# First projections for all 512 tokens in one pass, and the queries of three token blocks together

## The chip, the cores and the metric

The kernel runs on one core of a Trainium2 chip. The core has a TensorE for matrix products (PE in the profile), a VectorE (DVE), a ScalarE (ACT), a GpSimd (POOL), a SyncE (SP) that issues most transfers, and 16 DMA engines. The metric is the time of one execution on the device in microseconds (us).

## The reference, cut to what matters

512 tokens (T) of 1024 features (D) pass through two layers, all in float32. The first layer:

```python
mod = silu(c) @ w_ada + b_ada                       # 6 x 1024 modulations, one vector for all tokens
shift1, scale1, gate1, shift2, scale2, gate2 = split(mod, 6)
h = rms_norm(x, g1) * (1 + scale1) + shift1
q_g, k_g, v_g, a_lr, r_g, q_s, k_s, v_s = split(h @ w_in)    # the "first projections"
o_gla = rms_norm(gated_linear_attention(q_g, k_g, v_g, log_sigmoid(a_lr @ w_a + b_a) / 16)) * silu(r_g)
o_swa = rms_norm(sliding_window_attention(q_s, k_s, v_s))
x = x + gate1 * (concat(o_gla, o_swa) @ w_out)

h2 = rms_norm(x, g2) * (1 + scale2) + shift2
q = h2 @ w_peer_q                                   # 8 heads, two half queries of 128
s1, s2 = q_half1 @ keys_1.T, q_half2 @ keys_2.T     # 128 scores each
# 16 best of s1, 16 best of s2, then the 16 best of their 256 sums: 16 of 16,384 experts for each head
a = gelu(h2 . u_tab[expert]);  x = x + gate2 * sum(gate * a * v_tab[expert])
x = rms_norm(x, final_g)
```

The second layer takes x on: a norm, projections, differential and stick-breaking attention, an output projection, and a gated feed-forward layer. The output is x of all tokens.

## The kernel before

The tokens are four blocks of 128 (0 to 3), with features on the partitions and tokens along the free dimension. Two ways of computing the experts stand side by side. For blocks 0 and 3 (`SPARSE`), GpSimd gathers the chosen experts' rows, 128 of the up table (`peer_u`) and 128 of the down table (`peer_v`) per block, each gathered row 128 x 1024 floats (0.52 MB); VectorE consumes each row with one multiply-and-sum (`sparse`, 1191). For blocks 1 and 2 (`DENSE`), TensorE multiplies the 256 tokens with the whole tables, 128 steps each (`dense_u` 1314, `dense_v` 1381); the gates go into a 128 x 128 matrix per token (`gate_matrix`, 1258) that passes through DRAM.

A float32 product runs on TensorE as it stands, or as a "pair": ScalarE writes a rounded high part (`whi`), VectorE the rest (`wlo`, "a cut"), and `mm3` (393) makes three faster products of them. In the trace a float32 product leaves two records, a product of a pair one each.

The order of work on each engine is made as the program is built. `Model` (74) keeps a rough clock of the engines, and `Weaver` (225) always takes the next step of that generator whose last step ends first by it; a generator can wait for a key, for data, or stand back by a number of us. The constants from 52 on set how far parts stand back: `WIN` the projections of block 0, `SWL` the sliding window, `GLL` the linear attention of the later blocks. The product i of the up table for i of at least `AHEAD + SPILL` (17 + 32) waits for product i - `AHEAD` of the down table; the first `SPILL` activations go out to DRAM (`act_d`) and come back (`aR`) when the down table wants them. All instructions bear line 221, where a wrapper records them, so tiles tell them apart.

The front of the program, in which the change lies: `ada` (533) sums 48 groups of 128 modulations on VectorE, each over a 128 x 1024 piece of `w_ada`; 16 must be there before `first_norm` (574) can make its operand. The first projections (`w_in`, 604) run twice over 19 weight tiles: for block 0 in float32 (128 columns), then for blocks 1 to 3 in pairs (384 columns), so the weights are loaded twice. `gla` (705) runs the linear attention for block 0, for 1 and 2, and for 3; each has eight levels that end in two masked copies (`COPY_PREDICATED`), and ends in outputs `yT<-orb,b_w`, for which the gates (`silu` of r_g) must be there. `swa` (864) is the sliding window, `w_out` (977) the output projection, of block 0 and of blocks 1 to 3. `queries` (998) makes the second norm, the 16 tiles of queries and the scores: for block 0, for blocks 1 and 2 (256 columns), and for block 3, each in float32 and each with its own load of the weights. `topk_first` and `topk_second` (1084, 1099) search the scores; after block 0's the gathers of its experts begin.

The two lines that run all this:

```python
gla(pat, 0, 1, 0), [late(GLL)], gla(pat, 1, 3, 1), gla(pat, 3, 4, 1)   # of the call at 1511
W.run(posts(), topk(), gate_matrix(), dense_u(), dense_v(), until=("XD", "X0"))
```

## Time and profile before

| | |
|---|---|
| median of 3 runs | 2233.68 us (2230.89 to 2234.12) |
| span of the profiled execution | 2237.0 us |
| TensorE busy | 2040.0 us, 91% |
| VectorE busy | 1787.4 us, 80% |
| ScalarE busy | 968.8 us, 43% |
| GpSimd busy | 628.3 us, 28% |

The profile is of one execution of its own; its span is 3.3 us above the median of the timed runs. The busy shares are averages over stages that differ: where the program waits is seen only when the span is cut into stretches, and there for each engine's busy time, for the granted clock of TensorE and for the share of the time in which the DMA engines move data. A row of the time line is one instruction, or a run of like ones (x16), with its start, its duration, its engine, and the tiles out and in; what stands in brackets is how long the engine had been idle and what ended that. A row of the chain of waits is a piece of the path that ended last.

### The profile page before, as it was taken

The numbers are of one execution on the slowest core, as the hardware profiler recorded it, in microseconds if no ns is written. First come the engines' busy times: TensorE is split into PE (matmuls) and PEld (weight loads), VectorE is DVE, ScalarE is ACT, GpSimd is POOL, SyncE is SP. The second block draws the span as 40 slices with busy tenths as digits, with TensorE's granted clock in tenths as the row PEclk, the third lists the DMA queues.
The fourth block names the chain that finished last, engine by engine and source line by source line (L and its number), as shares of the span: only waits on it lengthen the run. The fifth ranks groups of instructions, "written<-read, shape, count | busy, mean of one in ns | idle before, by whom it ended". The sixth has DMA issues, their size and how long they took to land.

```text
span 2237.0 us, 36437 instructions
## 1 busy us (share of the span) xinstructions
PE 2040.0 (91%) x13373; PEld 1865.9 (83%) x13373; DVE 1787.4 (80%) x3723; ACT 968.8 (43%) x1824; POOL 628.3 (28%) x523
## 2 busy tenths in 40 slices
PE   2889899798999888999999999699997999999998
PEld 2778776687899788999999999587865999999887
DVE  6845897698999878888888697988978999932487
ACT  1331432212577533444444544445454333344376
POOL 0000223432112244333333133455522655400000
PEclk9899999799999988999999999899997999999999
DMA  9853447898898999999999798798855999954387
GB/s 367 335 207 129 160 146 240 278 326 312 281 325 304 358 337 321 366 344 354 343 374 330 241 380 292 272 326 289 286 178 159 371 354 364 356 166 139 130 306 268
DMA packets 227570, 638.32 MB, mean 285 GB/s; under 512 B 21264, under 2 KB 71712, under 8 KB 227392
## 3 DMA queue, kind: packets, MB, share of 16 engines
q1 hardware_dynamic: 153664, 367.54, 46.4%
q0 software_dynamic: 73728, 268.47, 34.1%
q8 instruction: 105, 1.72, 0.3%
q14 instruction: 73, 0.60, 0.1%
HBM read 611.54 MB, written 24.38 MB: 284 GB/s over the span
## 4 chain that ended last, share of the span: by engine, by line
PE 72%; DVE 11%; DMA 10%; ACT 3%; issue 3%; SPq 1%; POOL 0%; ACTq 0%; DVEq 0%; POOLq 0%
PE b_mm L221 46%; PE b_dacc L221 12%; PE b_w L221 6%; PE b_z L221 3%; DMA wraw<-peer_v 3%; DVE row L221 3%; DVE wlo L221 2%; DMA row<-w_up 1%; DMA aR<-act_d 1%; PE b_osb L221 1%; ACT whi L221 1%; SPq L221 1%; DMA row<-w_ada 1%; PE b_s L221 1%; DVE xT L221 1%
## 5 line engine op out<-in xcount | busy, mean ns | idle before, releaser
L221 POOL DMA_INDIRECT row<-peer_u,eU x256 | 311.4, 1217 | 845.7 <-DVE sm L221 250.1
L221 POOL DMA_INDIRECT row<-peer_v,eU x256 | 314.1, 1227 | 475.8 <-DVE vacc L221 204.6
L221 PE MATMUL b_mm<-u,whi 128*128 128x384 f32 x1216 | 327.4, 349 | 20.3 <-DMA sgt<-sgt 10.0
L221 PE MATMUL b_mm<-h,whi 128*128 128x256 f32 (+2 forms) x1632 | 329.9, 298 | 2.3 <-ACT whi L221 2.3
L221 DVE SCALAR_TENSOR_TENSOR vacc<-row,dots,vacc 128x1024 f32<-128x1024 f32 x254 | 324.7, 1278 | 3.9 <-DMA row<-peer_v,eU 3.5
L221 PE MATMUL b_dacc<-ghi,vhi 128*128 128x256 f32 x1024 | 296.0, 289 | 28.8 <-ACT ghi L221 28.7
L221 DVE SCALAR_TENSOR_TENSOR row<-row,h2n 128x1024 f32<-128x1024 f32 x256 | 309.8, 1218 | 13.1 <-DMA row<-peer_u,eU 13.0
L221 PE MATMUL b_dacc<-glo,vhi 128*128 128x256 f32 x1024 | 296.8, 290 | 2.4 <-DVE glo L221 1.8
L221 PE MATMUL b_dacc<-ghi,vlo 128*128 128x256 f32 x1024 | 294.7, 288 | 0.0
L221 PEld LDWEIGHTS b_mm<-h,whi 128*128 128x128 f32 (+1 forms) x1632 | 258.6, 190 | 8.9 <-issue 5.0
L221 PEld LDWEIGHTS b_mm<-u,whi 128*128 128x128 f32 x1216 | 223.5, 193 | 41.0 <-ACT u L221 20.4
L221 PE MATMUL b_mm<-h,wlo 128*128 128x256 f32 (+2 forms) x816 | 239.8, 294 | 8.7 <-DVE wlo L221 8.7
L221 PEld LDWEIGHTS b_dacc<-ghi,vhi 128*128 128x128 f32 x1024 | 201.1, 196 | 30.6 <-ACT ghi L221 30.5
L221 PE MATMUL b_mm<-u,wlo 128*128 128x384 f32 x608 | 209.0, 344 | 12.3 <-DVE wlo L221 12.3
L221 ACT ACTIVATE whi<-wraw 128x1024 fp32r<-128x1024 f32 (+5 forms) x143 | 128.0, 896 | 198.7 <-PE b_mm L221 112.2
L221 ACT ACTIVATE vhi<-wraw 128x1024 fp32r<-128x1024 f32 x128 | 136.0, 1063 | 169.5 <-PE b_dacc L221 100.6
L221 PEld LDWEIGHTS b_dacc<-glo,vhi 128*128 128x128 f32 x1024 | 201.1, 196 | 5.0 <-DVE glo L221 5.0
L221 PEld LDWEIGHTS b_dacc<-ghi,vlo 128*128 128x128 f32 x1024 | 201.6, 197 | 0.0
L221 PE MATMUL b_mm<-h,uraw 128*128 128x256 f32 x720 | 171.4, 386 | 4.6 <-DMA uraw<-peer_uT 3.2
L221 PEld LDWEIGHTS b_mm<-h,wlo 128*128 128x128 f32 (+1 forms) x816 | 156.2, 191 | 11.1 <-DVE wlo L221 10.3
L221 DVE TENSOR_TENSOR vlo<-wraw,vhi 128x1024 fp32r<-128x1024 f32 x128 | 156.1, 1220 | 10.5 <-PE b_dacc L221 9.9
L221 PEld LDWEIGHTS b_mm<-h,uraw 128*128 128x128 f32 x720 | 135.1, 195 | 21.7 <-issue 3.6
(350 smaller groups left out, 3787.2 us busy)
## 6 DMA issues: line engine op xcount, KB each, us to landing
uraw<-peer_uT SPq DMA_DIRECT2D x128, 512.0 KB
wraw<-peer_v SPq DMA_DIRECT2D x128, 512.0 KB
wraw<-w_in SPq DMA_DIRECT2D x60, 512.0 KB
row<-w_ada SPq DMA_DIRECT2D x48, 512.0 KB
wraw<-w_peer_q SPq DMA_DIRECT2D x32, 512.0 KB
gt<-gate_d SPq DMA_DIRECT2D x16, 1024.0 KB
gate_d<-stg SPq DMA_DIRECT2D x16, 896.0 KB
row<-w_in SPq DMA_DIRECT2D x24, 512.0 KB
```

The source lines that it names most:

```text
L221: return f(*args, **kw)
```

## The change

1. **First projections once.** x is loaded whole (two transfers of 1 MB) ahead of the modulations' weights, not block 0 first. `ada` takes the modulations in the order scale, shift of chunk 0, of chunk 1, and so on; as a pair is summed, `first_norm` makes that chunk (128 features) of the operand for all 512 tokens. `w_in` runs once over its 19 tiles, in pairs of 512 columns, and the weights are loaded once. Its first four tiles are cut in advance, their parts standing in room that belongs to q, k and v of the linear attention, and go chunk by chunk into four banks. `first_norm`, `gla` and `swa` lose the argument that told the two passes apart.
2. **Queries together.** `w_out(0, 1)`, `queries(0, 1)`, `w_out(1, 4)` and `queries(1, 4)` follow each other in one generator. The queries of blocks 1 to 3 are made in one go, in pairs of 384 columns (`pairs`, new), and w_peer_q is loaded twice, not three times. Block 3's scores are copied to SBUF. `topk_first` takes a group of heads of one block at a time; `topk_second` works in two halves of the heads.
3. **Order.** `AHEAD` 9 and `SPILL` 48 (57 in sum, before 49); `SWL` and `GLL` 0; `dense_u` waits for the output projection and takes pairs only once the queries are done (`post`) and VectorE is free by the model. The model's costs for TensorE and VectorE are other ones. `o1`, `o2` of the gate matrix have 2 buffers, not 3.

Counted over the program: 18 fewer loads of `w_in`, 16 fewer of `w_peer_q`, 8 fewer transfers of `w_out`; 16 more activations out to `act_d` and back; 55 steps of the up table in float32 and 73 in pairs, before 45 and 83. Gathered rows that VectorE has consumed when the last output projection stands, when the first product of the down table does, and at the end of the tables: before 47, 134 and 300, now 1, 103 and 284. Comments are gone from the file.

```diff
-AHEAD = 17
-SPILL = 32
+AHEAD = 9
+SPILL = 48
...
-    def w_in(b0, b1):
-        c, n = slice(128 * b0, 128 * b1), 128 * (b1 - b0)
+    def w_in():
...
+        pss = [bank(k) for k in ("mm", "mm", "s", "s")]
+        for kc in range(KC):
+            yield need(f"n{kc}")
+            for i in range(4):
+                mm3(pss[i], [x[:, kc] for x in spl[i]], (h1[:, 0, kc], h1[:, 1, kc]), kc == 0, kc == KC - 1)
+            yield at(M.free["PE"])
...
+    def pairs(tiles, xs, p, raw, n):
...
+        for i, (_, m, ev, *keys) in enumerate(tiles):
+            for k in keys:
+                yield need(k)
+            cut_hi(i + 1)
+            w = spl.pop(i)
+            ps = bank("mm")[:m, :n]
+            for kc in range(KC):
+                mm3(ps, (w[0][:, kc], w[1][:, kc]), (xs[0][:, kc], xs[1][:, kc]), kc == 0, kc == KC - 1)
+                if kc == 3:
+                    yield at(M.free["PE"])
+                    cut_lo(i + 1)
+                    load(i + 4)
...
-        yield need("Y")
+        yield need("x1")
+        stY.close()
...
-            if i < NE and ("G" in W.done or i >= AHEAD + SPILL - 2):
+            if i < NE and "post" in W.done and ("G" in W.done or i >= AHEAD + SPILL - 2 or
+                                                M.free["DVE"] < M.free["PE"] + USLACK):
...
+    def mixing():
+
+        yield late(FIRST0)
+        yield from w_out(0, 1)
+        yield from queries(0, 1)
+        yield late(0.0)
+        yield from w_out(1, 4)
+        yield from queries(1, 4)
+        W.set("post")
```

TensorE at its start, before (`h2n` is block 0's operand, `wraw` a weight tile, `ss` a constant, b_... the banks):

```order
L221 MATMUL b_sc<-yT,ones 128x128
L221 MATMUL b_mm<-h2n,wraw 128x128 x8
L221 MATMUL b_mm<-wraw,h2n 128x128 x8
L221 MATMUL b_mm<-h2n,wraw 128x128 x8
L221 MATMUL b_w<-ss,osq 128x512
L221 MATMUL b_w<-ss,osq 128x128
L221 MATMUL b_w<-ss,osq 128x512
L221 MATMUL b_w<-ss,osq 128x128
L221 MATMUL b_sc<-yT,ones 128x384
L221 MATMUL b_mm<-h2n,wraw 128x128 x8
```

And now (`h_143` holds both parts of the operand of all tokens; the cut weights of the first four tiles stand in `h2n` and `wlo`, `vg` and `kg`, `vg` and `qg`):

```order
L228 MATMUL b_w<-yT,ones 128x512 x8
L228 MATMUL b_mm<-h_143,h2n 128x512 x2
L228 MATMUL b_mm<-h_143,wlo 128x512
L228 MATMUL b_mm<-h_143,h2n 128x512 x2
L228 MATMUL b_mm<-h_143,wlo 128x512
L228 MATMUL b_s<-h_143,vg 128x512 x2
L228 MATMUL b_s<-h_143,kg 128x512
L228 MATMUL b_s<-h_143,vg 128x512 x2
L228 MATMUL b_s<-h_143,qg 128x512
```

Whole tiles of eight products of 128 columns have become products of 512 columns, a chunk of all four tiles at a time.

GpSimd from the state of the linear attention on, before (two `PT` tiles are cleared as a group of `gla` starts; a DMA of `peer_u` is a gathered row):

```order
L221 MEMSET state 128x512
L221 MEMSET PT_590 128x2x128
L221 MEMSET PT_591 128x2x128
L221 DMA row<-peer_u,eU 128x1024 x8
L221 MEMSET PT_1973 128x512
L221 MEMSET PT_1974 128x512
L221 DMA row<-peer_u,eU 128x1024 x26
L221 MEMSET PT_2793 128x2x128
L221 MEMSET PT_2794 128x2x128
L221 DMA row<-peer_u,eU 128x1024 x30
```

And now:

```order
L228 MEMSET state 128x512
L228 MEMSET PT_996 128x2x128
L228 MEMSET PT_997 128x2x128
L228 MEMSET PT_1568 128x512
L228 MEMSET PT_1569 128x512
L228 MEMSET PT_2119 128x2x128
L228 MEMSET PT_2120 128x2x128
L228 DMA row<-peer_u,eU 128x1024 x64
```

The gathers of block 0 stood between the groups of the linear attention; all of them stand behind the start of the third group now.

TensorE from the output projection of the later blocks (`yT`) into the queries, before (`wraw` a tile of the query weights, `h_3146` the operand in float32, `keys` the key table, `uraw` a piece of the up table):

```order
L221 MATMUL b_mm<-yT,wraw 128x128 x32
L221 MATMUL b_mm<-h_3146,ones 128x256
L221 MATMUL b_mm<-h_3146,wraw 128x256 x12
L221 MATMUL b_sc<-keys,qT 128x128 x2
L221 MATMUL b_mm<-h_3146,wraw 128x256 x8
...
L221 MATMUL b_mm<-h_3146,wraw 128x256 x4
L221 MATMUL b_mm<-h_3146,uraw 128x256 x4
```

And now (`h` is the operand in two parts, `vacc` block 0's operand, and `row` its query weights):

```order
L228 MATMUL b_mm<-vacc,row 128x128 x8
L228 MATMUL b_sc<-keys,qT 128x128 x2
L228 MATMUL b_mm<-yT,wraw 128x384 x64
L228 MATMUL b_mm<-h_2748,ones 128x384
L228 MATMUL b_mm<-ident,h_2748 128x128 x8
L228 MATMUL b_mm<-h,whi 128x384 x2
L228 MATMUL b_mm<-h,wlo 128x384
L228 MATMUL b_mm<-h,whi 128x384 x2
L228 MATMUL b_mm<-h,wlo 128x384
L228 MATMUL b_mm<-h_2748,uraw 128x256 x4
```

The output projection now has the last of block 0's queries ahead of it and 384 columns, and the queries behind it are pairs of 384 columns where they were float32 of 256.

## Rows read from the trace of the kernel before

**Rows 1.** Busy time by stretch, TensorE's granted clock, DMA share and rate:

```profile
core 0: us, PE busy (x) PEld busy (x) DVE busy (x) ACT busy (x) POOL busy (x), PEclk, DMA share, GB/s
0.00:50.00 50.00, 9.69 (x47) 9.21 (x48) 33.25 (x77) 8.78 (x12) 1.23 (x7) 0.95 0.98 370
50.00:421.00 371.00, 325.28 (x1912) 266.93 (x1911) 273.02 (x790) 117.13 (x272) 59.85 (x56) 0.90 0.61 208
421.00:573.00 152.00, 139.96 (x785) 124.70 (x786) 133.87 (x503) 35.97 (x84) 47.61 (x44) 0.96 0.87 311
573.00:780.00 207.00, 195.97 (x1171) 179.31 (x1170) 192.83 (x673) 142.05 (x343) 46.17 (x44) 0.97 0.92 322
780.00:906.00 126.00, 104.00 (x755) 100.50 (x756) 98.12 (x146) 43.88 (x65) 52.06 (x31) 0.88 0.95 330
906.00:1422.00 516.00, 511.25 (x4262) 509.66 (x4260) 436.30 (x581) 246.22 (x377) 163.88 (x135) 0.99 0.93 335
1422.00:1963.00 541.00, 494.31 (x2600) 440.21 (x2600) 478.80 (x735) 230.47 (x415) 257.51 (x207) 0.95 0.83 294
```

**Rows 2.** The time line of the first 60 us:

```profile
33.68 1.23 DVE L221 SCALAR_TENSOR_TENSOR row<-row,vacc 128x1024 f32<-128x1024 f32 x1
...
36.78 3.78 PE L221 MATMUL b_mm<-h2n,wraw 128*128 128x128 f32 x16 [24.11 <-DMA row<-w_ada]
...
40.35 2.59 PE L221 MATMUL b_mm<-wraw,h2n 128*128 128x128 f32 x16
```

**Rows 3.** The time line of TensorE near the end, products of 512 columns:

```profile
2136.06 0.40 PE L221 MATMUL b_odf<-whi,fh 128*128 128x512 f32 x1
...
2137.89 0.39 PE L221 MATMUL b_odf<-whi,fh 128*128 128x512 f32 x1
```

**Rows 4.** VectorE's instructions by tile and shape: count, busy us, mean ns, idle:

```profile
L221 DVE SCALAR_TENSOR_TENSOR vacc<-row,dots,vacc 128x1024 f32<-128x1024 f32 x254 | 324.7, 1278 | 3.9 <-DMA row<-peer_v,eU 3.5
L221 DVE SCALAR_TENSOR_TENSOR row<-row,h2n 128x1024 f32<-128x1024 f32 x256 | 309.8, 1218 | 13.1 <-DMA row<-peer_u,eU 13.0
...
L221 DVE TENSOR_TENSOR wlo<-wraw,whi 128x1024 fp32r<-128x1024 f32 x86 | 104.5, 1216 | 4.6 <-ACT whi L221 3.7 <-issue 0.9
```

**Rows 5.** The time line of VectorE and ScalarE through the linear attention:

```profile
99.72 0.77 DVE L221 COPY_PREDICATED PT<-masks,b_w 128x256 f32<-128x256 uint8 x2
...
125.08 0.77 DVE L221 COPY_PREDICATED PT<-masks,b_w 128x256 f32<-128x256 uint8 x2
...
136.22 0.69 DVE L221 TENSOR_TENSOR yT<-orb,b_w 128x512 f32<-128x512 f32 x1
...
273.92 1.34 DVE L221 COPY_PREDICATED PT<-masks,b_w 128x512 f32<-128x512 uint8 x2
...
310.24 1.34 DVE L221 COPY_PREDICATED PT<-masks,b_w 128x512 f32<-128x512 uint8 x2
...
345.11 1.48 ACT L221 ACTIVATE yT<-yT 128x1536 f32<-128x1536 f32 x1
...
351.23 0.69 DVE L221 TENSOR_TENSOR yT<-orb,b_w 128x512 f32<-128x512 f32 x1
...
359.82 0.69 DVE L221 TENSOR_TENSOR yT<-orb,b_w 128x512 f32<-128x512 f32 x1
...
370.86 0.76 DVE L221 COPY_PREDICATED PT<-masks,b_w 128x256 f32<-128x256 uint8 x2
...
397.43 0.77 DVE L221 COPY_PREDICATED PT<-masks,b_w 128x256 f32<-128x256 uint8 x2
...
407.52 0.69 DVE L221 TENSOR_TENSOR yT<-orb,b_w 128x512 f32<-128x512 f32 x1
```

**Rows 6.** The chain of waits, pieces of TensorE: start, us, what:

```profile
618.61 0.89 PE b_w L221 x8
619.50 1.73 PE b_mm L221 x8
...
1961.35 4.17 PE b_mm L221 x24
```

More of the change, by code (lines that the diff above doesn't have):

```diff
@@ L200, in call @@
                 fast = args[1].dtype == F32R and n >= 256
-                m.run("PE", n * 0.000425 if fast else max(n, 32) * 0.0017, [out], rest, rows=args[1].shape[0])
+                m.run("PE", n * 0.000417 + 0.013 if fast else max(n, 32) * (0.00167 if op == "matmul" else 0.00083) + 0.01, [out],
+                      rest,
+                      rows=args[1].shape[0])
             elif op == "preload_act_table_set":
@@ L361, in _emit, with load_ada @@
     wada = {}
-    def load_ada(i, i1):
-        if i < i1 and i not in wada:
-            wada[i] = pS.tile([128, D], F32, name="row", bufs=5)
-            SP.dma_start(wada[i], A["w_ada"][i])
+    ADA = [i + o for i in range(8) for o in (8, 0)] + list(range(16, 48))
+    def load_ada(n):
+        if n < 48 and n not in wada:
+            wada[n] = pS.tile([128, D], F32, name="row", bufs=ROWS)
+            SP.dma_start(wada[n], A["w_ada"][ADA[n]])
     cact = pX.tile([128, D], F32, name="vacc", bufs=1)
@@ L399, in _emit @@
     pool = {}
-    rings = {"w": (wp, "wraw", 4), "rows": (pS, "row", 5)}
+    rings = {"w": (wp, "wraw", 4), "rows": (pS, "row", ROWS)}
     def raw_tile(n=KC, m=128, ring="w"):
@@ L602, in ev_copy @@
         return f
-    def w_in(b0, b1):
-        c, n = slice(128 * b0, 128 * b1), 128 * (b1 - b0)
+    def w_in():
         def ev_nat(dst, key=None):
-            if b0 == 0:
-                f = ev_copy(dst[:, 0], key)
-                turned.add(f)
-                return f
             def f(ps):
-                yield from natural(dst, ps, pA, b1 - b0)
+                yield from natural(dst, ps, pA, 4)
                 if key:
@@ L995, in w_out @@
                             yT[:, k0:k1, c], 128 * (b1 - b0), ring="w" if b0 else "rows")
-        W.set(f"x{bounds[0]}")
+        W.set(f"x{b0}")
     def queries(b0, b1):
```

452 lines of the change are left out of this document (256 added, 196 removed).

## The prediction

> **What bounds the kernel now.** I read the busy times by stretch first: the run cut at points that both orders have [rows 1]. The cuts are the last output projection of blocks 1 to 3 (421 us), the end of the gate matrix and first product with the down table (780), the 33rd of these (906), the end of the tables (1422), and the last block's return from its experts (1963). From 573 to 780 VectorE and TensorE are both over 90% busy; from 780 to 906 TensorE has 104 of 126 us and the DMA queues 0.95; from 906 to 1422 TensorE has 511 of 516; from 1422 to 1963 TensorE has 494 and VectorE 479 of 541. The place with slack is the front: from 50 to 421 us TensorE has 325 and VectorE 273 of 371 us, the DMA queues 0.61. No one engine bounds the run: what is saved in front counts only if the later stretches, each full on another engine, do not take it back. So I sum five stretches against the profiled 2237 us and carry the difference over to the median.
>
> **Stretch 1, start to the last output projection: 421 before.** The projections begin with arriving data. Before, the last of 16 modulations is summed at 33.7 and the first product stands at 36.8 [rows 2]. Now all of x comes ahead of them, 1.57 MB more (384 tokens by 1024 by 4 bytes), at the 370 GB/s of the first slice [rows 1] 4.2 us: last modulation at 38. Behind it one chunk of the operand and 12 products of 512 columns; those start 0.229 us apart (eight steps from 2136.06 to 2137.89 [rows 3]), 2.7 us. With VectorE also cutting four weights (1.22 us each [rows 4]) and scaling x in that time, the first four tiles end near 47. Fifteen tiles remain, 24 products each: 15 x 24 x 0.229 = 82 us. Other rows of TensorE that the order puts among them (bias lines, 20 transposes, block 0's first two levels, the first scores) I put at 16 us: five products of 512 float32 columns at twice the 0.433 of 256 columns (four, two records each, take 1.73 [rows 6]) and some 55 of 128 columns at half of it. Projections end at 145. Before, they ran in two passes and the gates of blocks 1 to 3 came only at 345 [rows 5].
>
> Then the linear attention is a chain. Eight levels take 25.4 us for block 0, 36.3 for two blocks, 26.6 for the last; from the last level to the output 11.1 and 10.1; between two blocks' outputs 8.6; from an output to the next group's first level 11.0 [rows 5]. (Block 1's output at 351.2, 41 behind its levels, had waited for the gates; that goes.) In the new order six levels of block 0 stand behind the projections: 145 + 6 x 3.2 + 11 = 175; + 11 + 36 + 11 + 9 = 242; + 11 + 27 + 10 = 290. What is late next is TensorE: the rest of block 0's queries, four tiles of eight products of 128 columns, 7 us, stands ahead of the output projection, then 64 products of 384 columns in float32. One of 384 takes 1.5 x 0.433 = 0.65: 42 us. **Sum 339.** TensorE alone would give some 317 (the same float32 products without a wait). With every stall of before, from first level to output 36.5, 85.9 and 36.7, and block 0's first level at 133: 133 + 37 + 11 + 86 + 11 + 37 + 7 + 42 = 364. I take 339, since what stretched it, the late gates and the gathers' work on VectorE, is gone: gathers begin only after the third group's start (order of POOL) and 46 fewer rows are consumed by this point.
>
> On the clock: 50 to 421 us was granted 0.90, and the first eight products after the idle start took 3.78 us, the next eight 2.59 [rows 1, 2]. The Trainium skill (TensorE: Matmul & The Clock Gate, Part 1) says that the array's default is 1.2 GHz and that idle stretches bring it back there; it speaks against feeding TensorE chunk by chunk. The rows agree. Twelve products at half speed take 5.5 us, more than the 2.6 in which two modulations are summed (1.23 each [rows 2], and a read of each sum): eight chunks from about 20 us on would then end at 64 and not at 47, 17 us later. I keep 339 with that in the range.
>
> **Stretch 2, to the first product with the down table: 359 before.** VectorE was busy 133.9 + 192.8 = 327 us [rows 1]. Added: 16 cuts of the query weights, 16 x 1.22 = 19.5 [rows 4]; 15 more gathered rows consumed here (102 against 87, counted in VectorE's order), 15 x 1.25 = 19 (the two kinds take 1.22 and 1.28 [rows 4]); splitting three blocks instead of two and the searches in halves (some 20 more instructions a block), about 6. Removed: two cuts of the up table, 2.4. Sum 369, and at the 0.93 that VectorE has from 573 on, 397. TensorE was busy 336 and idle 23. Removed: block pair queries in float32, 128 x 0.433 = 55, and block 3's, half the columns, 28. Added: 384 products of 384 columns at 0.174 (24 in 4.17 [rows 6]), 67; ten more of the up table in float32, eight products each, 35, less two of its pairs at two thirds of 4.17, 6. So 349, the idle 23, and idle that is new. The norm of three blocks and not two ahead of the queries: half as much again of some 6, 3. And the last 19 steps of the gate matrix have no product of the table beside them, since its activations now end at 57: a step has 0.89 of its own and 1.73 of the table's [rows 6], so 19 x 1.73 = 33 if the steps keep their pace and nothing if VectorE, which makes their operands, has room; it has little, and I take 25. Together 400. Both engines say near **398**. Bounds: VectorE at 0.97, 380; TensorE with the whole 33 and 6 more, 414.
>
> **Stretch 3, tables: 642 before.** Product i of the up table waits for product i - AHEAD of the down table, so 33 of the latter ran alone before, in 126 us or 3.82 each [rows 1], and 49 do now: 187. The rest were 95 steps of the down table and 79 of the up table in 516 us, 2.97 each; now 79 + 71: 445. In all 632. Each of the 49 brings 0.52 + 0.13 MB and, by the order, one gathered row of 0.52: 57 MB and the gates' 6 in 187 us, 337 GB/s, what the rows show there. The rest would want about 156 MB in 445 us, 350 GB/s against 335, so I add 4: **636**, from 632 to 650.
>
> The DMA share there is 0.95 at 330 GB/s and 0.93 at 335 [rows 1]. The Trainium skill (DMA: Bandwidth & Descriptors, Bandwidth) gives 425 GB/s for a core whose neighbour is idle and about 358 when both stream; at the first figure the 49 would take 63 / 0.425 = 148 us. The rows do not bear that out, not even the 370 of the first slice reaches it. What a faster transfer would do, worked from rows, is the third rival.
>
> **Stretch 4, to the last block's return: 541 before.** Its mechanism is the late start of the gathers: at the end of the tables 284 rows have been consumed and not 300. The 16 that are left over cost VectorE 16 x 1.25 = 20 us where it has 62 idle of 541; and 78 products of the weaver move in from behind, 14 us of TensorE. At the pace of before (212 rows in 541) they would cost 41. I take 18: **559**, from 541 to 582.
>
> **Stretch 5: 274 before.** The 78 products of 0.174 are gone from it; some filled waits: 266, from 260 to 274.
>
> 339 + 398 + 636 + 559 + 266 = 2198, 39 below 2237; on the median of 2233.68 that is 2195.
>
> Covers: the 16 query cuts have ScalarE's halves beside them, on an engine that is busy 36 of 152 us from 421 on and 142 of 207 after that [rows 1]; the four copies of block 3's scores too. The 18 projection loads, 16 query loads and eight of the output projection that go (some 20 MB) shorten nothing by themselves, since the DMA share in front was 0.61; 16 more activations out and back (4 MB) are in stretch 3.
>
> **The rivals.** *The head start is kept whole.* Stretch 2 at 380 and stretch 4 at 541, for VectorE has room in both: 339 + 380 + 632 + 541 + 266 = 2158, median 2155. For it: 62 idle us in stretch 4. Against: VectorE at 93% from 573 on, and 15 more rows there.
>
> *Slower: the gathers set the end.* When the first down product starts, 103 rows have been consumed and not 134, so 409 are left and not 378. Those 378 took 1963 - 780 = 1183 us, 3.13 each, on VectorE and DMA queues near full. At that pace the last block returns at 737 + 409 x 3.13 = 2017, and with 266 behind it the run takes 2283, median 2280. My sum asks for 2.92 a row; it decides at (2237 - 266 - 737) / 409 = 3.02. For it: DMA shares of 0.93 to 0.95 from 780 to 1422. Against: the order puts the rows between the table's products, of which 8 fewer are left from 780 on (199, not 207), and VectorE has 80 idle us from 906 to 1422.
>
> *The transfers are not the limit of the lone down products.* Then TensorE sets their pace, 2.97 each as behind 906: 49 x 2.97 = 146 and not 187, so 2157 in all, median 2154. Against it: the 0.95.
>
> *The front does not come forward on the chip.* Stretch 1 at 364 and the chunks' 17 at half clock behind it: 2198 + 42 = 2240, median 2237: no difference.
>
> **How the numbers follow.** Forecast, 2165 to 2228: 0.62. Head start kept: 0.14. Slower: 0.14. Transfers not the limit: 0.03. No difference: 0.07. A measurement here tells 0.2%, 4.5 us. The forecast, the first and the third rival are faster: 0.79; same 0.07; slower 0.14. The range reaches from 2148, below the first rival, to 2243, which leaves out most of the slower one.
>
> **What would show it.** The windows of after: the last output projection near 339 and the first product with the down table near 737; VectorE above 90% between them and a TensorE gap at the end of the gate matrix; 49 down products in some 190 us at a DMA share of 0.95; tables done near 1373; the last block back near 1932. Wrong if the first of these points is past 378, if the stretch behind it is past 440, or if a gathered row takes over 3.02 us from the first down product to the last block's return.

## The result, and the profile after

The changed kernel takes 2256.6 us (median of 4 runs, 2254.4 to 2259.5) where the kernel before takes 2233.9: the ratio is 1.0116 with a 95% interval of 1.0093 to 1.0139. I had forecast 2195. It is slower by 1.2%, and outside my range of 2148 to 2243.

The profiled execution has a span of 2252.7 us. TensorE is busy 2017.5 us of it (2040.0 before), VectorE 1788.7 (1787.4), and 622 MB are moved (638): the change did remove work, and the time rose. The busy times by stretch, cut at the points of [rows 1] and finer between 369 and 931:

```profile
core 0: us, PE busy (x) PEld busy (x) DVE busy (x) ACT busy (x) POOL busy (x), PEclk, DMA share, GB/s
0.00:50.00 50.00, 24.06 (x68) 15.09 (x69) 29.98 (x49) 25.87 (x43) 1.23 (x7) 0.80 0.74 274
50.00:369.00 319.00, 289.64 (x1540) 214.09 (x1538) 213.94 (x707) 104.43 (x244) 7.37 (x10) 0.95 0.43 145
369.00:405.00 36.00, 15.47 (x50) 10.51 (x50) 24.28 (x36) 14.61 (x21) 10.50 (x8) 0.62 0.58 207
405.00:542.00 137.00, 133.86 (x725) 124.84 (x726) 104.43 (x303) 30.56 (x52) 62.94 (x50) 1.00 0.87 313
542.00:602.00 60.00, 53.20 (x246) 45.83 (x245) 53.41 (x244) 13.17 (x31) 11.47 (x11) 0.97 0.84 294
602.00:690.00 88.00, 85.97 (x506) 78.09 (x505) 85.53 (x366) 64.60 (x164) 11.15 (x11) 1.00 0.82 272
690.00:783.00 93.00, 70.15 (x415) 63.73 (x413) 89.10 (x326) 66.70 (x160) 14.29 (x14) 0.85 0.65 223
783.00:809.00 26.00, 0.58 (x1) 0.29 (x1) 11.73 (x17) 4.02 (x6) 11.50 (x10) 0.53 0.90 312
809.00:931.00 122.00, 103.12 (x756) 100.29 (x757) 96.05 (x144) 42.34 (x62) 47.52 (x31) 0.89 0.96 330
931.00:1435.00 504.00, 491.05 (x4068) 488.94 (x4068) 443.61 (x588) 236.17 (x362) 191.29 (x151) 0.98 0.97 355
1435.00:1990.00 555.00, 504.58 (x2677) 448.56 (x2677) 501.38 (x774) 235.43 (x422) 286.45 (x223) 0.96 0.85 304
1990.00:2252.70 262.70, 245.86 (x1773) 222.39 (x1771) 135.26 (x219) 137.86 (x249) 0.00 (x0) 1.00 0.60 205
```

By my five stretches:

| stretch | before | forecast | after |
|---|---|---|---|
| 1, to the last output projection | 421 | 339 | 369 |
| 2, to the first product with the down table | 359 | 398 | 438 |
| 3, the tables | 642 | 636 | 628 |
| 4, to the last block's return | 541 | 559 | 555 |
| 5, to the end | 274 | 266 | 263 |

Stretches 3, 4 and 5 came out within 10 us, the gathered rows consumed at the two cuts are the ones counted (103 and 285). The front did come forward, by 52 us. Stretch 2 grew by 79 and took all of it and more. In it, 369 to 809 above, VectorE is busy 368.5 us, which is the 369 of the forecast to the us, and TensorE 359 (349 forecast). What is wrong is the idle time: TensorE stands still for 81 us of 440, where I had 51 and where before it was 23 of 359.

Where TensorE stands still is in the rows: 20 us of 369:405, 7 of 542:602, 23 of 690:783 and 25 of 783:809. In 405:542 it is the other way round: TensorE has 134 of 137 and VectorE 104. The two engines are full in turns more than together. First TensorE makes the queries of three blocks with 17 steps of the up table between them, while VectorE stands idle 13 us for scores and 14 for gathered rows. Then VectorE searches and makes the gate matrix (602 to 783, 175 of 181 us); TensorE keeps up with it until 690 and runs out of work behind that, because the up table may only go 57 steps ahead.

Idle time alone does not say where the path grew. Cut at the first and the last gates that ScalarE copies out for DRAM, the stretch was 149 us to the first gates, 186 to the last and 24 to the first product with the down table before; it is 233, 182 and 24 now. So the whole growth lies ahead of the first gates: 20 us up to the first query (6 before, 25 now), and 70 from there to the last scores of the dense blocks, less 6 for the searches behind them. The middle piece, before and after:

```profile
426.80:507.00 80.20, 80.16 (x392) 70.93 (x392) 69.90 (x253) 15.51 (x34) 30.76 (x28) 0.98 0.86 311
393.80:544.00 150.20, 145.87 (x777) 135.20 (x778) 116.36 (x321) 31.92 (x53) 71.98 (x56) 0.98 0.86 307
```

TensorE is full in both. It has the columns of a third block in it now, and 18 float32 steps of the up table where it had 4; VectorE is busy 116 of 150 us where it was 70 of 80. Before, block 3's queries came behind these scores, beside the searches (507 to 575).

The first gap, the norm of three blocks ahead of the queries, in the chain of waits of after (start, us, what):

```profile
368.52 2.87 ACT h L228 x2
...
371.41 1.77 DVE h L228
...
374.90 1.64 PE b_mm L228 x2
...
378.38 1.15 ACT h L228 x2
...
386.68 1.15 ACT h L228 x2
```

ScalarE and VectorE hand the operand to each other in small steps for 26 us (368.5 to 394.4); before, the first product of a query started 6 us after the last output projection, now 25. The last gap, from the last gates to the first product with the down table:

```profile
783.74 6.42 DMA gate_d<-stg
...
790.81 6.21 SPq L228
...
797.06 9.76 DMA aR<-act_d
```

The gates go out to DRAM, and behind that the activations come back, 9.8 us: nothing else is ready for TensorE, since no step of the up table is allowed any more. Before, the same gap was as long (25 us, 755 to 780) and had 17 us of the up table's products in it. So the gap costs TensorE's time, and it does not put the first down product later than before.

### The profile page after: what moved, and what is told of

It reads as the page before. It is cut to its first block, busy times and chain, and to the rows that moved or that the text cites. A ratio compares the mean times of both kernels' runs of the same rounds, so it can differ in the third digit from the quotient of the medians.

```text
span 2252.7 us, 35362 instructions
## 1 busy us (share of the span) xinstructions
PE 2017.5 (90%) x12812; PEld 1812.7 (80%) x12812; DVE 1788.7 (79%) x3761; ACT 975.7 (43%) x1808; POOL 655.7 (29%) x523
## 4 chain that ended last, share of the span: by engine, by line
PE 59%; DVE 18%; DMA 12%; issue 5%; ACT 4%; POOL 1%; SPq 1%; ACTq 0%; DVEq 0%; POOLq 0%
PE b_mm L228 36%; PE b_dacc L228 11%; PE b_w L228 5%; PE b_z L228 4%; DMA wraw<-peer_v 3%; DMA row<-peer_v,eU 3%; DVE row L228 2%; DVE o L228 2%; DMA aR<-act_d 2%; DVE wlo L228 2%; DVE vacc L228 1%; POOL row L228 1%; DVE H L228 1%; PE b_osb L228 1%; DVE ti L228 1%
## 5 line engine op out<-in xcount | busy, mean ns | idle before, releaser
L228 POOL DMA_INDIRECT row<-peer_u,eU x256 | 324.4, 1267 | 643.9 <-DVE vacc L228 249.3
L228 POOL DMA_INDIRECT row<-peer_v,eU x256 | 328.4, 1283 | 413.1 <-DVE row L228 174.3
L228 PE MATMUL b_mm<-u,whi 128*128 128x384 f32 x1216 | 322.8, 345 | 19.8 <-ACT u L228 17.1
L228 PE MATMUL b_mm<-h,whi 128*128 128x256 f32 (+1 forms) x1424 | 288.3, 297 | 4.2 <-ACT qT L228 2.3
L228 PE MATMUL b_mm<-h,wlo 128*128 128x256 f32 (+2 forms) x848 | 264.2, 312 | 4.2 <-DVE wlo L228 4.2
L228 PEld LDWEIGHTS b_mm<-h,whi 128*128 128x128 f32 x1424 | 227.8, 191 | 7.1 <-ACT qT L228 3.6
L228 PE MATMUL b_mm<-h,uraw 128*128 128x256 f32 x880 | 202.8, 383 | 5.3 <-DMA uraw<-peer_uT 5.3
L228 ACT ACTIVATE whi<-wraw 128x1024 fp32r<-128x1024 f32 (+4 forms) x140 | 125.4, 897 | 189.2 <-PE b_mm L228 111.1
L228 PEld LDWEIGHTS b_mm<-h,uraw 128*128 128x128 f32 x880 | 165.8, 192 | 26.4 <-issue 6.0
L228 PEld LDWEIGHTS b_mm<-h,wlo 128*128 128x128 f32 x848 | 160.3, 189 | 13.2 <-DVE wlo L228 5.9
```

What stands on the lines that cost most here:

```text
L228: return f(*args, **kw)
```

## The experiments

In the table, x1 is the last output projection, V0 the first cut of a tile of the down table, XD the end of the tables, "rows left" the gathered rows not yet consumed at XD, X3 the last block's return; all from the profiled execution of each run, in us. The ratio is against the kernel before, timed beside each run (its medians went from 2228.5 to 2233.9 us). `after` and a_nochunk have the same instructions in the same order on the four engines that compute, and lie 4 us apart in the median and 8 in end - XD; a smaller difference between two rows is not read as one.

| run | x1 | V0 | XD | rows left | X3 - XD | end - XD | ratio (95%) |
|---|---|---|---|---|---|---|---|
| before | 421 | 780 | 1422 | 211 | 541 | 815 | |
| after | 369 | 808 | 1435 | 227 | 555 | 818 | 1.0116 (1.0093 to 1.0139) |
| b_order | 421 | 801 | 1436 | 210 | 539 | 817 | 1.0072 (1.0044 to 1.0100) |
| b_lategather | 405 | 766 | 1397 | 256 | 650 | 907 | 1.0348 (1.0320 to 1.0376) |
| a_spill64 | 369 | 821 | 1420 | 239 | 584 | 841 | 1.0161 (1.0132 to 1.0190) |
| a_f32q | 372 | 810 | 1435 | 223 | 555 | 822 | 1.0101 (1.0073 to 1.0129) |
| a_split | 366 | 773 | 1400 | 251 | 607 | 862 | 1.0200 (1.0174 to 1.0227) |
| a_nochunk | 370 | 809 | 1431 | 227 | 561 | 826 | 1.0101 (1.0081 to 1.0120) |
| a_skew0 | 367 | 799 | 1425 | 227 | 553 | 819 | 1.0081 (1.0060 to 1.0102) |
| a_front | 369 | 808 | 1437 | 227 | 554 | 817 | 1.0118 (1.0092 to 1.0144) |
| a_pace2 | 368 | 821 | 1445 | 194 | 487 | 807 | 1.0128 (1.0104 to 1.0153) |
| a_minus16 | 367 | 806 | 1434 | 211 | 520 | 813 | 1.0086 (1.0063 to 1.0110) |
| a_mix | 368 | 779 | 1410 | 215 | 527 | 817 | 1.0003 (0.9985 to 1.0021) |
| b_best | 399 | 762 | 1400 | 216 | 532 | 815 | 0.9918 (0.9893 to 0.9942) |
| b_best2 | 400 | 765 | 1407 | 212 | 530 | 814 | 0.9949 (0.9933 to 0.9966) |
| b_best3 | 397 | 759 | 1402 | 217 | 531 | 807 | 0.9898 (0.9871 to 0.9924) |

I began with two theories: S, that the new numbers of the tables' order (57 activations, 49 lone down products) cost the time; and L, that the gathers' later start does (the first gathered row is consumed at 366 us, at 258 before).

### b_order: the tables' numbers alone, in the kernel before

```diff
-AHEAD = 17
-SPILL = 32
+AHEAD = 9
+SPILL = 48
```

> The kernel before with one part of the change alone: AHEAD 9 and SPILL 48 in place of 17 and 32. Theory S (the short cover: activations that end at 57 and the lone down products are what costs): eight more float32 steps of the up table, 8 x 3.46 = 28 us of TensorE, stand ahead of the down table where TensorE is full, and eight fewer pairs behind it give back about 8 x 2.2 = 17; with a dead gap at the gates' round trip of up to 20 us the median comes to 2245 to 2260. Theory L (late gathers: block 0's gathers start 107 us later, so 46 rows of VectorE work move from the slack front into full stretches): this part costs little, 2228 to 2245.

Measured 2247.6 us, 1.0072. V0 comes 21 us later, XD 14, the end 15. The busy times to V0:

```profile
601.00:755.00 154.00, 153.97 (x911) 140.81 (x910) 150.31 (x558) 105.44 (x261) 32.00 (x31) 0.99 0.94 319
755.00:801.00 46.00, 28.46 (x186) 26.44 (x185) 27.05 (x33) 13.58 (x21) 17.96 (x14) 0.83 0.96 359
```

TensorE was full to 755 and then had 28 of 46 us, the gap that S speaks of. So in the kernel before these numbers cost 15 us by themselves. That is not a part of the 23 us of the whole change: here the gate matrix ends when it did (757 us, 756 before), and it is 44 us from there to V0, because the last steps of the up table stand behind it and wait for loads. In the changed kernel those steps are done by 739 us, ahead of the last gates, and the same piece takes the 24 us of before.

### b_lategather: late gathers alone, in the kernel before

```diff
         yield need(f"E{b}")
+        yield need("x1")
         acc = pX.tile([128, D], F32, name="vacc", bufs=1)
```

> The kernel before with the gathers of block 0 held until the last output projection of blocks 1 to 3 (421 us in place of 253), nothing else. Theory L: 47 rows move behind 421, 47 x 1.25 = 59 us of VectorE work into stretches that have some 20 to 60 us of VectorE idle: 2260 to 2285. Theory S: the rows find room in the idle of VectorE behind the tables and the median stays below 2245.

Measured 2307.0 us, 1.0348, more than L's upper end. But where it is lost speaks against L as I had put it:

```profile
405.00:766.00 361.00, 336.49 (x1948) 304.59 (x1947) 329.10 (x1216) 171.10 (x407) 97.59 (x89) 0.95 0.89 316
766.00:1397.00 631.00, 606.58 (x4978) 602.93 (x4978) 533.86 (x697) 279.69 (x423) 220.32 (x167) 0.97 0.95 342
1397.00:2047.00 650.00, 535.23 (x2843) 480.35 (x2844) 550.34 (x857) 243.99 (x443) 324.27 (x251) 0.91 0.82 288
2047.00:2304.00 257.00, 231.30 (x1643) 208.04 (x1641) 124.65 (x201) 133.37 (x243) 0.00 (x0) 0.96 0.56 193
```

x1, V0 and XD all come earlier (405, 766, 1397), by 14 to 25 us, with VectorE freed; the whole loss lies behind the tables, where 256 rows are left instead of 211, and 650 us pass before the last block returns. In the changed kernel end - XD is as short as before (818 and 815).

### a_spill64: more activations ahead, in the changed kernel

```diff
-SPILL = 48
+SPILL = 64
```

> The changed kernel with SPILL 64 in place of 48, nothing else: up to 16 more float32 steps of the up table may run ahead of the down table. Theory S: they fill the 48 us that TensorE is idle from 690 us to the first down product, and each takes a step of 2.97 out of the full stretch behind and puts 0.8 into the lone down products: 16 x 2.2 = 35 us less, 2222 to 2236. Theory L: VectorE sets the pace up to the end of the gate matrix, the extra steps delay it or find only the 26 us of the round trip, 2240 to 2256.

Measured 2265.1 us, 1.0161: slower than the changed kernel, which neither theory had. The tables end 15 us earlier, as S says, but only 273 rows have been consumed by then and not 285, and end - XD grows from 818 to 841.

### a_f32q: the queries not in pairs

```diff
-        if not b0:
-            yield from gemm(tiles, h2, n, ring="rows")
-        else:
+        if True:
+            yield from gemm(tiles, h2, n, ring="w" if b0 else "rows")
+        else:
```

> The changed kernel with the queries of blocks 1 to 3 in float32 products of 384 columns, not in pairs: TensorE gets 128 x 0.65 = 83 us in place of 67, VectorE loses 16 cuts of 1.22, 20 us, ScalarE as many. If VectorE sets the time from the output projection to the first down product, as theory L has it, the median falls by 5 to 20 us, to 2237 to 2252; if TensorE sets it (theory S), it rises by 10 to 18, to 2266 to 2275.

Measured 2254.2 us against 2256.6 of the changed kernel: no difference. That the queries are in pairs moves work from TensorE to VectorE and neither gains nor loses. That each engine waits for the other in this stretch would explain it, and is not shown.

### a_split: block 3's queries apart again

```diff
-        yield from queries(1, 4)
+        yield from queries(1, 3)
+        yield from queries(3, 4)
...
-        if not b0:
-            yield from gemm(tiles, h2, n, ring="rows")
+        if b0 != 1:
+            yield from gemm(tiles, h2, n, ring="w" if b0 else "rows")
```

(With it the operand's tiles are of 256 columns, and block 3's scores stay in the banks.)

> The changed kernel with one part undone: the queries of blocks 1 and 2 go first, in pairs of 256 columns, and those of block 3 behind them in float32, with their weights loaded again, as in the kernel before. Theory Q (the queries of three blocks in one go put block 3's share and its norm ahead of the dense blocks' searches, so the gate matrix starts at 602 us and the down table at 808): the gate matrix starts 30 to 40 us earlier, the first down product stands near 775, and the time falls with it, 2222 to 2237. Theory L (gathered rows set the end, at some 1.6 us for each that is not consumed in time): the first down product comes earlier, but fewer rows are consumed by then and by the tables' end, and the last block returns no earlier: 2250 to 2275.

Measured 2272.3 us (2263 to 2278), 1.0200. Both theories had their half:

```profile
366.00:773.00 407.00, 359.36 (x2218) 327.75 (x2218) 352.44 (x1310) 177.71 (x396) 82.31 (x78) 0.94 0.82 281
773.00:1400.00 627.00, 593.38 (x4824) 588.50 (x4824) 542.98 (x723) 275.45 (x423) 255.13 (x182) 0.97 0.97 353
1400.00:2006.00 606.00, 530.61 (x2805) 473.34 (x2805) 539.91 (x837) 239.86 (x428) 322.54 (x247) 0.94 0.86 306
2006.00:2261.00 255.00, 231.99 (x1644) 208.78 (x1642) 125.34 (x202) 133.64 (x243) 0.00 (x0) 0.96 0.57 194
```

V0 stands at 773 (808 in the changed kernel) and the tables end 35 us earlier, at 1400, as theory Q says: with block 3's share out of the way the first gates are copied out at 551 and not at 602, 186 us behind x1 and not 233. It was 149 before, so 36 us of that remain with the queries apart. But 251 rows are left then, and the last block returns 607 us later. The end is 9 us later than the changed kernel's in the profile, 16 in the medians.

### a_nochunk: an edit that did not reach the chip's order

```diff
-            yield need(f"n{kc}")
+            yield need("n7")
```

> The changed kernel with the first four tiles of the projections not begun chunk by chunk: their 96 products of 512 columns, 96 x 0.229 = 22 us, wait for the last chunk of the operand. If the start is worth what my stretch 1 says, the fifth tile starts some 11 us later (it stood at 65), and so do the last output projection and the gathers: 2262 to 2275. If the start of the front does not reach the end: within 4 us of the changed kernel, 2253 to 2261.

Measured 2252.9 us, 0.17% from the changed kernel. The edit tells only the planner to wait; TensorE's instructions stand in the same order as without it, and each still starts when its own chunk is there (the first at 35.2 us). So it says nothing of the chunks; it shows how far two runs of the same instructions lie apart.

### a_skew0: more one-hots on ScalarE

```diff
-SKEW = 2
+SKEW = 0
```

> The changed kernel with more of the gate matrix's one-hots made on ScalarE (SKEW 0 in place of 2: ScalarE takes them as soon as it is free before VectorE), nothing else. ScalarE is idle 49 of 181 us there and VectorE 6. If VectorE sets the pace of the gate matrix: its end comes 5 to 10 us earlier and so does the first down product; the time falls by as much or, where rows set the end, by less: 2246 to 2254. If TensorE or the one-hots' buffers set the pace: 2254 to 2262.

Measured 2246.7 us, 10 us less than the changed kernel and 6 less than a_nochunk, which was timed beside it: the gate matrix ends 9 us earlier, V0 and XD as much, and the end with them. VectorE does set the pace of the gate matrix, and with 227 rows left, what comes off ahead of XD comes off the end, us for us.

### b_best: a middle between the two kernels

```diff
-        ("G", 3.0, None), ("Y", 2.0, None), ("gla3", 2.0, None), ("gla1", 4.0, None), ("", 6.0, None))
+        ("G", 3.0, None), ("Y", 2.0, None), ("gla3", 4.0, None), ("gla1", 4.0, None), ("", 6.0, None))
...
-WIN = 8
+WIN = 12
...
-WL = 3
+WL = 0
```

(And the changed kernel's costs of TensorE and VectorE in `Model`.)

> The kernel before with the order alone changed: the costs that the change gives TensorE and VectorE in the order's model, the projections of blocks 1 to 3 not held back (WL 0, not 3), those of block 0 a little later (WIN 12, not 8), the gathers held back 4 us and not 2 behind the linear attention. Block 0's search then ends later than before (by some 75 us in the order) and the last output projection comes some 15 us earlier: a middle between the two kernels. Theory L: the late gathers cost 1.6 us for each row that is not consumed in time, and the front gives 15 to 20 back: 2225 to 2260. If what comes earlier in front is worth its full time and later gathers cost nothing: 2205 to 2218.

Measured 2213.6 us, 0.9918. The gathers start 80 us later than before, 31 of the 47 rows are not yet consumed at x1, and yet it is faster: L's price of 1.6 us for each late row is wrong. XD is 23 us earlier with 216 rows left, and end - XD is the 815 of before.

### a_minus16: 16 rows less

(The last 16 gathered rows of the down table for block 3 are left out, their gathers and their products.)

```diff
-        tabs += [("peer_v", i) for i in range(64, 128)]
+        tabs += [("peer_v", i) for i in range(64, 112 if b == 3 else 128)]
```

> The changed kernel without the last 16 gathered rows of the down table for block 3 (left out: their gathers and their products), so that as many rows are left at the end of the tables as in the kernel before, 211, where the change left 227. Theory L (the rows that are left set the end): 16 rows at the 2.44 us that a row takes there, 39 us less: 2210 to 2226, back at the kernel before or below. If TensorE or the later start of the tables sets the end: at most 10 us less, 2246 or more.

Measured 2249.3 us: 7 us less than the changed kernel (4 less than a_nochunk) and not 39. L falls here.

```profile
1434.00:1955.00 521.00, 470.86 (x2479) 415.40 (x2478) 469.49 (x741) 222.50 (x400) 271.59 (x207) 0.96 0.84 300
1955.00:2247.00 292.00, 279.19 (x1969) 256.59 (x1969) 159.79 (x244) 152.68 (x273) 0.00 (x0) 1.00 0.59 199
```

The last block does return 34 us earlier, at 1955, but what follows takes 293 us and not 263. From the end of the tables to the end TensorE is busy 471 + 279 = 750 us, as in the changed kernel (505 + 246) and before (494 + 260), and the time from there to the end, 813 us, is near the 818 of the changed kernel: rows that come sooner only move that work about. In some 65 of these us TensorE stands idle; what sets that was not followed up.

### a_front: VectorE's first instructions in another order

```diff
         raws.update(ahead)
+        yield need("gs1")
...
         yield data(rn)
+        yield need("gs1")
```

> The changed kernel with VectorE's first instructions in another order: four sums of modulations ahead of the cuts of the first weights, and the scaling of x behind them; before, the second sum stood at 28.5 us behind cuts that waited for ScalarE. If that order is why the last of 16 modulations came at 52 and not at 38: it comes at 44 to 47, the projections end 5 to 8 us earlier (165 to 168, before 172), and the last output projection too. The time falls by 3 to 8 if the front reaches the end, 2248 to 2254, and by less than 4 if the rows alone count.

Measured 2255.5 us, as the changed kernel. The last of 16 modulations came at 48.8 and not at 51.9, the projections ended at 165.8 and not at 171.7, and block 0's output of the linear attention came at 205.6 and not at 211.4; but block 1's came at 267.4 and not at 266.4, and the last output projection stood at 368 as in the changed kernel. The 6 us are lost between 205 and 268 us. TensorE is busy 58 of these 63 us in both runs, at a granted clock of 0.84 here and 0.95 in the changed kernel; that this is the reason is not shown.

### a_pace2: gathers less held back

```diff
-        ("G", 3.0, None), ("gla3", 4.0, None), ("gla1", 4.0, None), ("", 6.0, None))
+        ("G", 3.0, None), ("gla3", 2.0, None), ("gla1", 2.0, None), ("", 2.0, None))
```

> The changed kernel with its gathers held back less: 2 us in the order where they stood back 4 and 6 up to the end of the linear attention and behind it. Rows are consumed earlier, and the searches, the gate matrix and the tables come later by 10 to 25 us. Theory L alone (each row in hand is worth 2.4 us at the end of the tables): 30 to 40 more rows there, 70 to 95 us, less the 20 by which the tables end later: 2180 to 2215. If TensorE's work behind the tables sets the end as soon as the rows do not: 2235 to 2275.

Measured 2255.4 us, no difference. 33 more rows are in hand at XD (194 left), the last block returns at 1932 and not at 1990, and the 310 us of TensorE's work behind it fill the 319 us to the end. From XD to the end it is 11 us less than in the changed kernel, and XD comes 10 later. At 2.4 us a row 33 rows would be 80 us, so with a_minus16 this is the second run in which fewer rows left are worth little.

### b_best2: one-hots on ScalarE, in the middle kernel

```diff
-SKEW = 2
+SKEW = 0
```

(on top of b_best)

> As b_best, and more of the gate matrix's one-hots on ScalarE (SKEW 0, not 2), which took 10 us off the changed kernel: VectorE is as full in the gate matrix here, so 3 to 10 us below b_best (2213.6): 2203 to 2211. If the gate matrix of this order is not bound by VectorE: 2211 to 2218.

Measured 2218.3 us, 0.9949: a miss. The gate matrix ends 4 us earlier, but V0 comes 3 us later and XD 7. What helped the changed kernel does not help here: from the last gates to V0 it is 37 us where b_best has 30, and two loads of pieces of the up table stand in the path there, which land at 739 and 762 us. Why they come later was not followed up.

### a_mix: the front kept, the queries apart, the rows not given up

```diff
-SKEW = 2
+SKEW = 0
...
-SPILL = 48
+SPILL = 44
...
-("dv3a", 1.0, "DVE"), ("ua", 1.0, None), ("V127", 0.5, None),
-("gla3", 4.0, None), ("gla1", 4.0, None)
+("dv3a", 1.0, "DVE"), ("ua", 0.5, None), ("V127", 1.0, None),
+("gla3", 2.0, None), ("gla1", 1.0, None)
```

(on top of a_split; the lines of `PACE` are shown by their entries)

> The changed kernel with the queries of blocks 1 and 2 ahead of block 3's again (as in a_split), and the order's numbers set so that gathered rows are not given up for it: gathers held back 2 us behind the linear attention, not 4, and 1 us behind the tables' start, not 0.5; SKEW 0; SPILL 44. New theory (two limits): the time is the end of the tables plus the larger of 815 us, which TensorE takes behind it with its 750 us of work, and 2.45 us for each row left then plus 263. a_split had the tables' end at 1400 but 251 rows left. Here both: tables done near 1408 with at most 225 rows left, so 2215 to 2232, 25 to 40 below the changed kernel; the front's gain is there once the queries stand apart. Theory of the front (what the first projections gain is lost in the front itself): no better than 2240.

Measured 2229.8 us, 1.0003, inside the range of the two limits:

```profile
368.00:779.00 411.00, 345.21 (x2130) 312.19 (x2130) 368.48 (x1266) 210.56 (x499) 126.00 (x110) 0.93 0.89 316
779.00:1410.00 631.00, 602.18 (x4919) 598.21 (x4919) 549.92 (x749) 285.75 (x434) 253.21 (x185) 0.97 0.98 354
1410.00:1938.00 528.00, 479.43 (x2511) 425.28 (x2511) 476.71 (x738) 226.13 (x410) 267.61 (x211) 0.95 0.84 301
1938.00:2227.00 289.00, 274.80 (x1940) 252.09 (x1939) 157.03 (x240) 149.81 (x263) 0.00 (x0) 1.00 0.59 199
```

The tables end at 1410 with 215 rows left, and the rest takes 817 us. It is 27 us faster than the changed kernel and as fast as the kernel before, by four edits together, which are not told apart. Of the 53 us that x1 is ahead of before, 12 are left at XD: x1 to V0 takes 411 us here, with VectorE busy 368 as in the changed kernel, where before it was 327 of 359.

### b_best3: near the point where rows begin to count

```diff
-SPILL = 32
+SPILL = 28
```

(on top of b_best)

> As b_best, with SPILL 28 in place of 32: four fewer steps of the up table ahead of the down table. b_best had 216 rows left at the end of the tables (1399.5), 11 below the 225 at which rows begin to count. Two limits: an earlier first down product (by 5 to 10 us) and about the same end of the tables, within 7 us of 1399, so 2205 to 2216; more rows than 225 left would make it later than 2220.

Measured 2206.1 us, 0.9898 (0.9871 to 0.9924): the fastest of all, 1% below the kernel before.

```profile
397.00:759.00 362.00, 323.92 (x1875) 292.77 (x1875) 327.26 (x1197) 173.56 (x418) 98.19 (x90) 0.94 0.88 311
759.00:1402.00 643.00, 623.85 (x5111) 620.08 (x5111) 563.25 (x760) 294.47 (x449) 250.59 (x188) 0.98 0.96 353
1402.00:1932.00 530.00, 481.06 (x2549) 425.44 (x2549) 480.26 (x741) 227.14 (x409) 271.31 (x213) 0.96 0.84 303
1932.00:2208.00 276.00, 266.47 (x1900) 244.36 (x1898) 147.48 (x234) 147.95 (x263) 0.00 (x0) 1.00 0.61 204
```

217 rows are left at XD and it takes 807 us from there, so the rows do not count yet.

### What the runs say together

The time is the end of the tables plus the larger of two: some 815 us of TensorE's work and idle time behind it (807 to 826 in the thirteen executions with 194 to 227 rows left, of which it is busy 747 to 754 where I summed it), and 2.42 to 2.54 us for each row left plus 255 to 257 (841, 862 and 907 us at 239, 251 and 256 rows). The kernel before and the changed one are both on the first branch, the changed one at its edge. So its loss is the later end of the tables, 13 of the 16 us between the two spans, and that comes from stretch 2. In three pieces, from the traces (us; the gates are copied out by ScalarE):

| run | x1 to the first gates | first to last gates | last gates to V0 |
|---|---|---|---|
| before | 149 | 186 | 24 |
| b_order | 149 | 187 | 44 |
| after | 233 | 182 | 24 |
| a_split | 186 | 191 | 31 |
| a_mix | 200 | 189 | 23 |

Not tried alone are the two buffers of the one-hots, where there were three, and the other numbers of the order; the gate matrix, which uses these buffers, takes no longer than before.

## Why the prediction was wrong, by its own steps

**Stretch 1: right in kind, 30 us too short.** The projections ended at 172 and not at 145; from there to the last output projection it took 197 us where I had 194. The sum of that chain held, with luck: block 0's output came 40 us behind the projections and not 30, and the two later groups took less than I had. The first term that was mis-sized is the start. I let the modulations come as fast as the transfers, 38 us; the 16th was summed at 52. VectorE's first instructions in the changed kernel (start, us, and in brackets the idle time before and what ended it):

```profile
11.19 1.23 DVE L228 SCALAR_TENSOR_TENSOR row<-row,vacc 128x1024 f32<-128x1024 f32 x1 [8.48 <-DMA row<-w_ada]
...
20.29 2.36 DVE L228 TENSOR_TENSOR wlo<-wraw,h2n 128x1024 fp32r<-128x1024 f32 x2 [7.87 <-ACT h2n L228]
22.57 1.22 DVE L228 TENSOR_TENSOR kg<-wraw,vg 128x1024 fp32r<-128x1024 f32 x1
23.71 4.90 DVE L228 TENSOR_TENSOR yT<-xT,rn 128x512 f32<-128x512 f32 x8
28.52 1.21 DVE L228 SCALAR_TENSOR_TENSOR row<-row,vacc 128x1024 f32<-128x1024 f32 x1
```

and ScalarE's, on which the second row waits:

```profile
17.69 0.69 ACT L228 ACTIVATE rn<-b_w,eps 128x512 f32<-128x512 f32 x1 [4.37 <-PE b_w L228]
...
19.22 1.99 ACT L228 ACTIVATE h2n<-wraw 128x1024 fp32r<-128x1024 f32 x2
```

VectorE takes its instructions in order: after one sum, at 11.2, it waits for a cut whose first half ScalarE makes at 19.2, behind the norm's factor at 17.7; then it scales x, and the second sum stands at 28.5. The sums free the buffers for the next weights, so the transfers stop as well: SyncE waits for a sum for up to 14.8 us. Share (tenths) and rate of the DMA queues in 40 slices of the first 70 us, after and before:

```profile
DMA  0799999999995000044389999999999999999449
GB/s 0 211 433 407 417 405 421 417 410 410 412 396 225 0 0 0 0 103 197 80 276 337 360 396 353 272 307 375 377 377 356 356 325 308 372 370 386 190 80 382
```

```profile
DMA  0788999999999999999999999999999690799479
GB/s 0 200 295 222 417 419 419 400 407 412 407 407 412 410 405 393 396 414 410 412 407 401 376 380 389 330 376 410 412 407 389 204 334 33 197 309 405 180 119 347
```

The slices with 0 from 22.7 to 29.8 us are the cost. I had named the cuts and the scaling as work beside the sums and not seen that they stand ahead of them. So the first chunk's products started at 34.6 where I had some 20, and from 36.4 TensorE was never idle until the four tiles were done, at 60.6 and not 47: 14 of the 30 us. The fifteen tiles and the other rows among them took 111 us and not 98, with TensorE busy 104: 13 more. Whether the 14 reach the last output projection is not settled: a_front mended 6 us of the projections' end, and the last output projection did not move.

**The clock at the start: some 2 us, and not the 17 of my range.** TensorE's products of the first four tiles, and the first behind them:

```profile
38.67 1.05 PE L228 MATMUL b_s<-h,vg 128*128 128x512 f32 x2
...
43.65 0.63 PE L228 MATMUL b_mm<-h,h2n 128*128 128x512 f32 x2
...
59.71 0.63 PE L228 MATMUL b_s<-h,vg 128*128 128x512 f32 x2
...
65.15 1.11 PE L228 MATMUL b_mm<-ident,vT 128*128 128x128 f32 x4 [4.57 <-ACT vT L228]
```

Two products are 1.05 us at 38.7 and 0.63 at 43.7: the granted clock was 0.53 from 34.6 to 40.8 us, behind 17 us of idle time, and 1.00 from there to 60.5. The first chunk took 4.5 us from 36.4 on where the next took 2.8, so it cost some 2 us. For the 17 I had every chunk at the lower level; but the products followed each other without a gap. Once more, behind a wait of 4.6 us, the clock was 0.50 from 65.1 to 70. The Trainium skill (TensorE: Matmul & The Clock Gate, Part 1) says that the array's default is 1.2 GHz; the trace agrees, but the 17 us for it are not there.

**Stretch 2: the step that failed.** The two sums of busy time were right (VectorE 369 and 368.5; TensorE 349 and 359). What failed is how I turned them into time: "at the 0.93 that VectorE has from 573 on, 397". That share held where both engines had work at once: from the first gates to the last VectorE has 0.96 of the time (0.97 before). Ahead of the first gates it has 0.78, where it had 0.88. Putting three blocks' queries together takes the overlap away: block 3's queries were what TensorE did beside the dense blocks' searches, and they stand ahead of the scores now, in the 150 us in which VectorE is busy 116. Beside the searches TensorE does steps of the up table, which it lacks at the end of the gate matrix. So the gate matrix starts 233 us behind x1 and not 149. a_split shows a part of it: apart again, the first gates come 186 us behind x1, and x1 to V0 is 407 us and not 439, though not the 359 of before. I had the last 19 steps of the gate matrix without cover as 25 us (23 measured); they left the gate matrix no longer than before. Of the norm I had 3 us more, and TensorE stands idle 20 ahead of the first query, 15 more than before. The idle time of the round trip (25 us, 8 before) I did not have, but the trip itself is no longer, so it is no part of the 79. VectorE had 42 us more to do here than before, mostly rows and cuts, as forecast. Of the 84 us by which the first gates come later behind x1, 20 are the norm and 70 the queries up to the dense blocks' last scores, less 6 of the searches. How the 70 divide between block 3's columns, the 14 more steps of the up table (49 us of TensorE at 3.46 each) and the wait of queries for searches is not settled.

**Stretch 3: right.** The 49 lone down products took 184 us (187 forecast), the rest 443 (445 and 4).

**Stretches 4 and 5: right in size, wrong in mechanism.** 818 us against 825. I priced the 16 rows left over at 18 us of VectorE; in a_minus16 they are worth 4 to 7, near the noise, and stretch 5 grew by what stretch 4 lost: TensorE's 750 us had to be done behind the tables in either case.

**The rivals.** "The gathers set the end" was to decide at 3.02 us a row from V0 to the last return; it was (1990 - 808) / 409 = 2.89, so it fell, though the kernel is slower. The head start was not kept. The lone products took 184 us (330 GB/s at a share of 0.96) and not the 146 of the third rival, and the front did come forward, by 52 us. The slower case that came true was none of mine: two stretches that each missed, by 30 and 40 us, which my range did not take together. That the last three came out within 10 us each is part luck, since the limit that I gave stretch 4 was not the one at work.

## What to carry to other kernels

Before you turn the busy times of two engines into a time, look whether they have work at the same time: a change that batches what one engine hands to another (three blocks' queries in one go) can leave both sums as you forecast them and still add the waiting. Put work together only if what waited beside it is replaced; the share of a full stretch of before does not carry over. And look for the limit behind a point before you price what is left over there: here 194 to 227 rows made little difference to the time behind the tables, and from 239 on it was some 2.5 us for each of them.

## What the runs showed of the hardware

In the slices shown above the queues moved 405 to 433 GB/s from 3.5 to 19 us after the change, and 393 to 419 from 7 to 37 us before it, where I had taken the mean of a stretch, 370, as their best; in the tables they moved 330 to 355 GB/s at a share of 0.96 to 0.97. The Trainium skill (DMA: Bandwidth & Descriptors, Bandwidth) gives 425 GB/s for a core whose neighbour is idle; the trace agrees for whole loads in a row, and my forecast had taken it that no row bears that rate out. For the lone down products it changes nothing: there a share near 1 went with 330 GB/s.
